# Two delta-net convolution tiles in place of two z tiles in a mixer's lead GEMM, with the delta net's gates woven beside the other convolutions

## The chip, the cores and the metric

The kernel runs on one core of a Trainium2 chip. A core has TensorE (PE; its weight loads are listed apart as PEld), VectorE (DVE), ScalarE (ACT), GpSimd (POOL) and SyncE (SP), which in this kernel issues transfers only. The metric is the device time of one execution in microseconds (us), as a median over runs. The compiler lays out each engine's instructions in one queue ahead of time, and an engine takes its queue in order.

## The reference, cut to what matters

The network takes 512 tokens of width 1024 and has four layers: two of a first kind, each a mixer and a feed-forward part, and two of a second kind, which the change doesn't touch. A mixer is, cut:

```python
h = rmsnorm(x, norm_mix_g[l])
proj = h @ w_in[l]
(qa, ka, va, qd, kd, vd, beta_logit, decay_logit, z, gate_logit) = jnp.split(proj, offsets, axis=-1)
...
y_attn = grid_attention(qa, ka, va) @ w_o_attn[l]
qkv = jax.nn.silu(centred_depthwise_conv(jnp.concatenate([qd, kd, vd], axis=-1), dn_conv_w[l])).astype(f32)
...
beta = jax.nn.sigmoid(beta_logit.astype(f32)).reshape(b, s, 2, DN_HEADS)
g = -jnp.exp(dn_a_log[l].astype(f32)) * jax.nn.softplus(
    decay_logit.astype(f32).reshape(b, s, 2, DN_HEADS) + dn_dt_bias[l].astype(f32))
o = bidir_gated_deltanet(qd, kd, vd, beta, g)
o = rmsnorm(o, dn_out_norm_g[l]) * jax.nn.silu(z.astype(f32).reshape(b, s, DN_HEADS, DN_DV))
y_dn = o.reshape(b, s, DN_V).astype(x.dtype) @ w_o_dn[l]
gates = jax.nn.sigmoid(gate_logit).reshape(b, s, N_BRANCH, D_MODEL)
mixed = gates[:, :, 0] * y_attn + gates[:, :, 1] * y_dn
```

So z (512 columns, four tiles of 128) and the 2048 gate columns (sixteen tiles) are needed only at the end of a mixer, while the convolution of qd, kd, vd (1536 columns, twelve tiles) and beta and g (32 columns) are what the delta net begins with.

## The kernel before, in words

**GEMMs.** Activations lie feature by token. Every GEMM splits its operands in a high and a low part and makes three products. `wload` (L390) brings a weight tile from HBM to `st`; ScalarE copies the high part `wh`; VectorE, or for a share given by `aid` GpSimd, subtracts to `wl`. `g_fm` (L414) makes one PSUM tile of 128 features by 512 tokens with 24 matmuls (8 steps along the width of 1024, three products each), after each step yields a cost of 0.64, and at the end calls an evacuation. Its PSUM tiles come from the pool `pg` with three banks, and with one bank during the scan (`share_banks`, L135, which also finishes a background tile that was begun).

**Lead and follow.** The rms norm is one row R over the tokens, and it multiplies a GEMM's result rather than its input. So the first GEMM of a stage runs before R is known: `lead` (L177) takes two generators for eight steps each; `follow` (L195) runs them to their end, which is their evacuation. In a mixer the two are z tiles (`begin_mixer`, L1319; from `load_x` for the first layer, from the end of the FFN for the second), evacuated by `g_tanh` (L1254): tha = 0.5 * pg * R on VectorE, a tanh to thz on ScalarE, for z (but not for the gate tiles) a second VectorE operation, and a store from SP's queue.

**Background.** Tiles that are needed late are pushed on a list: the two other z tiles, then eight tiles `ga` and eight `gd` (L1339). `pull` adds the cost of each foreground step, times a ratio, to a debt, and steps the list while the debt is positive (L149 to L207). `pe` (L240) keeps background matmuls a fixed number of foreground instructions behind. `weave` (L219) interleaves streams by cost over weight.

**The delta net** (`delta_net`, L1272) has three stages:
- `prepare` runs with ratio R1[4] = 0.059, woven with the attention's row inputs (`g_grid_inputs`, weight R1[6] = 0.491). Within it come first the gates (`g_dn_gates`, L864: one GEMM of 32 columns into a `pg` bank, transposed products into `pa`, a softplus in many small VectorE operations, sums by small matmuls, gc, eg and kds, and a round trip through memory to the factors `fac`), then the convolutions of head group 0 (`g_dn_inputs`, L947; q, k, v of two tiles each), then those of group 1 woven with the decay tiles (`g_dn_decay`, L991, which read `fac`).
- the solve of both groups (`g_dn_solve`, L1012) runs with ratio R1[1] = 0.633.
- the scan of both groups and the attention run with ratio R1[2] = 0.45 and one `pg` bank.

After that all remaining background is run, and the output GEMMs follow.

**A convolution tile's evacuation** (`evac`, L956): VectorE writes pad = pg * R into one of two pad buffers, which frees the bank; ScalarE starts the sum (cva, a scaled copy); VectorE adds the four other taps (cva from pad, cols, cva); ScalarE takes a tanh (cvt); VectorE joins them (cva from cvt, cva); TensorE transposes four times into `pt`; ScalarE copies to the q, k or v tile; for q and k ScalarE squares and VectorE reduces (dnms). When all six tiles of a group are done, dnv and a short chain of small operations give the l2 norm's factor, and tmk and tmq are scaled.

R1 (L1904) = [2.071, 0.633, 0.45, 3.49, 0.059, 9.505, 0.491, 4.55, 0.469, 0.387, 0.519, 0.788]; the last three are GpSimd's shares of `wl` (for foreground and background up to the solve, and for background in it). The change leaves R1 as it is.

Of the kernel before, what the change touches and what calls it, by code (L numbers as in the profile page):

```python
# [11 lines left out]
AF = mybir.ActivationFunctionType  # L12
ALU = mybir.AluOpType
AX = mybir.AxisListType
# [5 lines left out]
T = 512  # L20
D = 1024
NT = 4
# [84 lines left out]
class Net:  # L107
    def __init__(self, tc, I, consts, out):
        self.tc, self.nc, self.I, self.out = tc, tc.nc, I, out
        self.consts = consts  # L110
        nc = tc.nc
        self.V, self.G, self.S, self.PE = nc.vector, nc.gpsimd, nc.scalar, nc.tensor
        self.n = 0
# [830 lines left out]
        self.act(gt, p4, AF.Exp)  # L944
        return beta3, fac, kds3, eg3, gt

    def g_dn_inputs(self, l, pool, ip, g):  # L947

        w = self.I["w_in"][l]
        out = {}  # L950
        ms = self.t(self.sm, [128, 2, NT, 4], "dnms")
        for kind in range(3):
            dst = self.t(pool, [128, NT, 256], "tm" + "qkv"[kind], bufs=2)
            out["qkv"[kind]] = dst

            def evac(i, ps, kind=kind, dst=dst):  # L956
                ft = 4 * kind + 2 * g + i
                c = [self.cols[:, 64 + 60 * l + 12 * j + ft : 65 + 60 * l + 12 * j + ft] for j in range(5)]
                p = self.pad[self.npad % 2]
                self.npad += 1  # L960
                self.tt(p[:, 2 : T + 2], ps, self.R, ALU.mult)
                a = self.t(ip, [128, T], "cva")
                self.act(a, p[:, 2 : T + 2], AF.Copy, scale=c[2])
                for j in (0, 1, 3, 4):
                    self.stt(a, p[:, j : j + T], c[j], a, ALU.mult, ALU.add)
                th = self.t(ip, [128, T], "cvt")
                self.act(th, a, AF.Tanh, scale=0.5)
                self.stt(a, th, 1.0, a, ALU.add, ALU.mult)
                pt = self.t(self.pt, [128, T], "pt")
                for t in range(NT):  # L970
                    self.tr(pt[:, 128 * t : 128 * t + 128], a[:, 128 * t : 128 * t + 128])
                p3 = pt.rearrange("p (t n) -> p t n", t=NT)
                self.act(dst[:, :, 128 * i : 128 * i + 128], p3, AF.Copy, scale=0.5 if kind == 2 else 1.0)
                if kind < 2:
                    sq = self.t(ip, [128, T], "cvt")
                    self.act(sq, pt, AF.Square)
                    self.V.tensor_reduce(ms[:, kind, :, 2 * i : 2 * i + 2],
                                         sq.rearrange("p (t h d) -> p t h d", t=NT, h=2), AX.X, ALU.add)

            yield from self.g_fm(w, D, 768 + 512 * kind + 256 * g, 256, self.xh, self.xl, evac, 128)  # L980
        v = self.small(32, "dnv", 2)
        self.V.tensor_scalar(v, ms.rearrange("p a t h -> p (a t h)"), 4 * EPS, None, ALU.add)
        r = self.small(32, "dnr", 2)
        self.rsqrt(r, v)
        self.V.tensor_scalar(r[:, 0:16], r[:, 0:16], 0.125, None, ALU.mult)
        for kind in range(2):
            a = out["qkv"[kind]].rearrange("p t (h d) -> p (t h) d", d=64)
            self.tt(a, a, bc(r[:, 16 * kind : 16 * kind + 16], 64), ALU.mult)
        return out
# [282 lines left out]
    def delta_net(self, l, od, inputs, attention):  # L1272

        pool, cm = self.pool(f"dn{l}", bufs=2)
        ep, ecm = self.pool(f"dne{l}", bufs=4, side="right")
        ip, icm = self.pool(f"dni{l}", bufs=4)

        def prepare():  # L1280
            G = yield from self.g_dn_gates(l, pool, ep, ip)
            x0 = yield from self.g_dn_inputs(l, pool, ip, 0)
            x1, E0, E1 = yield from self.weave(
                (self.g_dn_inputs(l, pool, ip, 1), 1.0), (self.g_dn_decay(l, ep, 0, G), R1[0]),
                (self.g_dn_decay(l, ep, 1, G), R1[0]),
            )
            return G, (x0, x1), (E0, E1)

        self.aid = R1[9], R1[10]
        (G, x, E), _ = self.run(prepare(), R1[4], (inputs, R1[6]))  # L1290
        icm.__exit__(None, None, None)
        self.aid = 0.0, R1[11]
        tp, tcm = self.pool(f"dnt{l}", bufs=2)
        sp, scm = self.pool(f"dns{l}", bufs=2)
        sol = self.run(
            self.g_dn_solve(l, tp, ep, sp, 0, x[0], E[0]), R1[1],
            (self.g_dn_solve(l, tp, ep, sp, 1, x[1], E[1]), 1.0),
        )
        for c in (scm, ecm):
            c.__exit__(None, None, None)  # L1300
        cp, ccm = self.pool(f"dnc{l}", bufs=2)
        ap, acm = self.pool(f"ga{l}", bufs=2)
        hp, hcm = self.pool(f"gh{l}", bufs=2, side="right")
        self.aid = 0.0, 0.0
        self.share_banks(True)
        self.pull(R1[8])
        _, _, oa = self.run(
            self.g_dn_scan(l, cp, 0, x[0], G, *sol[0], od), R1[2],
            (self.g_dn_scan(l, cp, 1, x[1], G, *sol[1], od), 1.0), (attention(ap, hp), R1[3]),
        )  # L1310
        self.share_banks(False)
        for c in (acm, ccm, tcm, cm):
            c.__exit__(None, None, None)
        return oa, hcm
# [3 lines left out]

    def begin_mixer(self, l):  # L1319
        self.zd = self.t(self.dr, [128, 4, T], f"zd{l}")  # L1320
        z = self.tanh_tiles(self.I["w_in"][l], 2336, 4, lambda f: self.zd[:, f, :], True)
        self.push("z", *z[2:])
        return [(g, 8) for g in z[:2]]

    def mixer(self, l):
        self.last = deque(self.last, maxlen=LAG[0])
        I = self.I
        w = I["w_in"][l]
        thd = self.t(self.dr, [128, 16, T], f"thd{l}")
        zd = self.zd  # L1330
        ad = self.t(self.dr, [128, 4, T], f"ad{l}")
        qd = self.t(self.dr, [128, 4, 2, T], f"qd{l}")
        kd = self.t(self.dr, [128, 2, 2, T], f"kd{l}")
        vd = self.t(self.dr, [128, 2, NT, 2, 64], f"vd{l}")
        gp, gcm = self.pool(f"mix{l}", bufs=2)
        self.gp = gp
        od = [self.t(gp, [128, 2, T], f"o{g}", bufs=1) for g in range(2)]
        self.follow()
        self.push("ga", *self.tanh_tiles(w, 2848, 8, lambda f: thd[:, f, :]))  # L1339
        self.push("gd", *self.tanh_tiles(w, 2848 + 1024, 8, lambda f: thd[:, 8 + f, :]))  # L1340

        def gate(f, ps, dst):
            th = self.t(dp, [128, T], "th", bufs=4)
            self.nc.sync.dma_start(th, thd[:, f, :])
            self.stt(dst, th, 1.0, ps, ALU.add, ALU.mult)

        inputs = self.g_grid_inputs(l, qd, kd, vd)
        oa, hcm = self.delta_net(l, od, inputs, lambda pool, hp: self.g_grid_attention(l, pool, hp, qd, kd, vd, ad))
        for name in ("z", "ga", "gd"):
            self.need(name)  # L1350
        pool, cm = self.pool(f"mo{l}", bufs=2)
        mx = self.f32r_tiles(pool, NK, "m")
        dp, dcm = self.pool(f"md{l}", bufs=2)
        self.selp = self.t(dp, [128, 4, 128], "selp", F32R, bufs=1)
        self.V.tensor_copy(self.selp.rearrange("p a b -> p (a b)"), self.const(dp, "selp", 128, 512, "sq"))
        o = self.f32r_tiles(dp, 4, "o")
        u = [self.t(dp, [128, T], f"u{f}", bufs=1) for f in range(NK)]

        def evac_d(f, ps):
            a = self.t(dp, [128, T], "sq")  # L1360
            gate(8 + f, ps, a)
            self.tt(a, a, u[f], ALU.add)
            self.split(mx[0][f], mx[1][f], a)


        norm = self.g_dn_out(l, dp, zd, od, o)
        part = self.g_fm(I["w_o_attn"][l], 512, 0, D, *oa, lambda f, ps: gate(f, ps, u[f]), 128)
        for n in (4, 8, 4):
            for _ in range(n):
                next(part)  # L1370
            self.after = next(norm)
        self.run(norm)
        self.run(part)
        self.after = None
        self.gemm_fm(I["w_o_dn"][l], 512, 0, D, *o, evac_d)
        dcm.__exit__(None, None, None)
        hcm.__exit__(None, None, None)
        self.residual(pool, I["w_out"][l], D, *mx, 0.5, self.col(1, l), lambda: self.begin_ffn(l))
        for c in (cm, gcm):
            c.__exit__(None, None, None)  # L1380
# [523 lines left out]
R1 = [2.071, 0.633, 0.45, 3.49, 0.059, 9.505, 0.491, 4.55, 0.469, 0.387, 0.519, 0.788]  # L1904
# [54 lines left out]
```

## Time and profile before

| | |
|---|---|
| median of 3 runs | 3095.34 us (3093.31 to 3095.86) |
| the profiled execution | 3096.09 us, of which its span is 3094.3 |
| mean granted TensorE clock of the profiled execution | 0.988 |
| PE, DVE, ACT, POOL busy, share of the span | 97%, 72%, 49%, 13% |

The profile is one execution of its own, 0.75 us above the median. Its times are in us unless marked ns; durations of matmuls overlap, since they are pipelined. A name such as pad or cva is a tile of the program; "out<-in" says what an instruction writes and reads; L254, L257 and L260 are the helpers through which all VectorE and ScalarE operations pass, so the tile tells them apart and not the line. The granted clock is a share of full speed.

### The profile page before, as it was taken

What the parts mean: (1) busy time and instruction counts of PE and PEld (TensorE: products, weight loads), DVE (VectorE), ACT (ScalarE), POOL (GpSimd) and SP (SyncE); (2) the same over time, 40 slices, a digit from 0 to 9 for tenths busy, and PEclk for the clock granted to TensorE, in tenths of its full rate; (3) what the DMA queues carried; (4) which work ended last, traced back from release to release, by engine and by line L of the source; (5) the groups of instructions that cost most, each with busy time, mean ns of one, the idle gap of its engine ahead of it and who ended that gap; (6) DMA issues with size and microseconds to landing.
All of it is one profiled execution on the core that took longest, in us unless ns stands there. A gap on an engine that the chain in (4) does not pass through costs nothing. (4 is left out here: it accounts for less than half of the span.)

```text
span 3094.3 us, 54458 instructions
## 1 busy us (share of the span) xinstructions
PE 3011.5 (97%) x20148; PEld 2540.6 (82%) x20148; DVE 2221.3 (72%) x4974; ACT 1502.0 (49%) x3043; POOL 416.4 (13%) x550
## 2 busy tenths in 40 slices
PE   8989999999999899999999999999999999999999
PEld 6877778888888777788888898888888898878977
DVE  5988776777448887777774466778686666788684
ACT  3544744444324456544443344366464453476463
POOL 2433300000014343100000000200100010200200
PEclk9999999999999999999999999999999999999999
DMA  4435125333343342253333454522435545422525
GB/s 146 115 90 146 43 88 175 96 99 96 125 129 89 106 120 85 68 167 107 98 98 123 136 140 131 143 75 73 123 113 186 158 118 150 121 66 67 162 87 183
DMA packets 403116, 359.02 MB, mean 116 GB/s; under 512 B 32867, under 2 KB 350307, under 8 KB 402851
## 3 DMA queue, kind: packets, MB, share of 16 engines
q1 hardware_dynamic: 396707, 335.62, 37.6%
q0 software_dynamic: 6144, 19.93, 1.8%
q8 instruction: 159, 2.61, 0.4%
q14 instruction: 106, 0.87, 0.1%
HBM read 293.98 MB, written 61.47 MB: 115 GB/s over the span
## 5 line engine op out<-in xcount | busy, mean ns | idle before, releaser
L260 ACT ACTIVATE wh<-st 128x512 fp32r<-128x512 f32 x844 | 528.2, 629 | 788.5 <-PE pg L238 633.4
L254 DVE TENSOR_TENSOR wl<-st,wh 128x512 fp32r<-128x512 f32 x766 | 539.0, 705 | 402.0 <-ACT wh L260 397.2
L238 PE MATMUL pg<-xh,wh 128*128 128x512 f32 (+1 forms) x1824 | 733.0, 402 | 3.6 <-ACT wh L260 2.2
L238 PE MATMUL pg<-xh,wl 128*128 128x512 f32 (+1 forms) x1824 | 719.9, 395 | 5.3 <-POOL wl L254 5.3
L238 PE MATMUL pg<-xl,wh 128*128 128x512 f32 (+1 forms) x1824 | 712.2, 395 | 0.0
L238 PEld LDWEIGHTS pg<-xl,wh 128*128 128x128 f32 (+1 forms) x1824 | 343.4, 188 | 73.8 <-issue 0.4
L238 PEld LDWEIGHTS pg<-xh,wl 128*128 128x128 f32 (+1 forms) x1824 | 344.2, 189 | 72.0 <-POOL wl L254 7.0
L238 PEld LDWEIGHTS pg<-xh,wh 128*128 128x128 f32 (+1 forms) x1824 | 344.2, 189 | 70.7 <-ACT wh L260 2.6
L238 PE MATMUL pg<-wl,xh 128*128 128x256 f32 x928 | 265.1, 287 | 0.4 <-DVE wl L254 0.4
L238 PE MATMUL pg<-wh,xh 128*128 128x256 f32 x928 | 262.6, 287 | 1.1 <-DVE oz L257 0.8
L238 PE MATMUL pg<-wh,xl 128*128 128x256 f32 x928 | 263.0, 285 | 0.0
L238 PEld LDWEIGHTS pg<-wh,xh 128*128 128x128 f32 x928 | 176.3, 192 | 6.2 <-DVE oz L257 1.0
L238 PEld LDWEIGHTS pg<-wl,xh 128*128 128x128 f32 x928 | 177.9, 192 | 3.9 <-DVE wl L254 0.8
L238 PEld LDWEIGHTS pg<-wh,xl 128*128 128x128 f32 x928 | 177.7, 192 | 1.2
L485 POOL DMA_DIRECT2D xd<-xn x40 | 21.8, 544 | 1049.5 <-DVE xn L257 927.5
L254 POOL TENSOR_TENSOR wl<-st,wh 128x512 fp32r<-128x512 f32 x78 | 123.1, 1584 | 267.5 <-ACT wh L260 234.4
L238 PE MATMUL pg<-hh,wl 128*128 128x512 f32 x352 | 137.0, 389 | 0.0
L238 PE MATMUL pg<-hh,wh 128*128 128x512 f32 x352 | 136.7, 389 | 0.0
L238 PE MATMUL pg<-hl,wh 128*128 128x512 f32 x352 | 135.7, 389 | 0.0
L260 ACT ACTIVATE p<-pa,anb 128x128 f32<-128x128 f32 (+1 forms) x224 | 115.6, 517 | 36.9 <-DVE anb L725 34.0
L257 DVE SCALAR_TENSOR_TENSOR u<-pad,cols,u 128x512 f32<-128x512 f32 x176 | 127.3, 746 | 0.7
L260 ACT ACTIVATE ph<-pt 128x128 fp32r<-128x128 f32 (+1 forms) x224 | 94.9, 426 | 65.9 <-PE pt L251 64.5
(509 smaller groups left out, 6276.2 us busy)
## 6 DMA issues: line engine op xcount, KB each, us to landing
st<-in_w_in_dram SPq DMA_DIRECT2D x400, 256.0 KB
st<-in_w_up_dram SPq DMA_DIRECT2D x176, 256.0 KB
st<-in_w_down_dram SPq DMA_DIRECT2D x88, 256.0 KB
st<-in_w_out_dram SPq DMA_DIRECT2D x64, 256.0 KB
xo<-xd SPq DMA_DIRECT2D x48, 256.0 KB
th<-thz SPq DMA_DIRECT2D x48, 256.0 KB
xd<-xn POOLq DMA_DIRECT2D x40, 256.0 KB, 4.0
thd<-thz SPq DMA_DIRECT2D x32, 256.0 KB
```

The source lines that it names most:

```text
L238: return self.pe(self.PE.matmul(out, lhsT, rhs, start=start, stop=stop, **kw))
L254: return (eng or self.V).tensor_tensor(out, a, b, op)
L257: return self.V.scalar_tensor_tensor(out, a, s, b, op0, op1)
L260: return self.S.activation(out, in_, f, **kw)
L485: self.nc.gpsimd.dma_start(self.xd[:, k, :], x)
```

## The change

- The lead GEMM of a mixer is two convolution tiles (q, tiles 0 and 1, which are head group 0's), not two z tiles. All four z tiles go to the background list, ahead of the gate tiles.
- The evacuation of a convolution tile and its GEMM become a function of their own, `g_conv`; `dn_tiles` makes a group's tiles. `g_dn_inputs` leaves out the first `led` tiles.
- `follow()` moves from `mixer` into `delta_net`, behind the opening of its pools, and so behind the pushing of the gate tiles.
- The gates are no longer run ahead of group 0's convolutions, but woven beside the four that are left, with weight 0.8 against 1.0.

```diff
-    def g_dn_inputs(self, l, pool, ip, g):
+    def g_conv(self, l, kind, f, dst, ms):
+        def evac(_, ps):
+            ft = 4 * kind + f
...
+            p = self.pad[self.npad % 2]
+            self.npad += 1
+            self.tt(p[:, 2 : T + 2], ps, self.R, ALU.mult)
+            a = self.t(self.conv_pool, [128, T], "cva")
...
         w = self.I["w_in"][l]
-        out = {}
-        ms = self.t(self.sm, [128, 2, NT, 4], "dnms")
+        return self.g_fm(w, D, 768 + 512 * kind + 128 * f, 128, self.xh, self.xl, evac, 128)
+
+    def dn_tiles(self, pool, g):
+
+        x = {k: self.t(pool, [128, NT, 256], "tm" + k, bufs=2) for k in "qkv"}
+        return x, self.t(self.sm, [128, 2, NT, 4], "dnms")
+
+    def g_dn_inputs(self, l, g, tiles, led=0):
+
+
+        out, ms = tiles
         for kind in range(3):
...
-            yield from self.g_fm(w, D, 768 + 512 * kind + 256 * g, 256, self.xh, self.xl, evac, 128)
+            for i in range(2):
+                if 2 * kind + i >= led:
+                    yield from self.g_conv(l, kind, 2 * g + i, lambda kind=kind: out["qkv"[kind]], lambda: ms)
...
         ip, icm = self.pool(f"dni{l}", bufs=4)
+        self.conv_pool = ip
+        self.conv_tiles = self.dn_tiles(pool, 0)
+        self.follow()
 
         def prepare():
-            G = yield from self.g_dn_gates(l, pool, ep, ip)
-            x0 = yield from self.g_dn_inputs(l, pool, ip, 0)
+            x0, G = yield from self.weave(
+                (self.g_dn_inputs(l, 0, self.conv_tiles, 2), 1.0), (self.g_dn_gates(l, pool, ep, ip), 0.8)
+            )
             x1, E0, E1 = yield from self.weave(
-                (self.g_dn_inputs(l, pool, ip, 1), 1.0), (self.g_dn_decay(l, ep, 0, G), R1[0]),
+                (self.g_dn_inputs(l, 1, self.dn_tiles(pool, 1)), 1.0), (self.g_dn_decay(l, ep, 0, G), R1[0]),
                 (self.g_dn_decay(l, ep, 1, G), R1[0]),
             )
...
         self.zd = self.t(self.dr, [128, 4, T], f"zd{l}")
-        z = self.tanh_tiles(self.I["w_in"][l], 2336, 4, lambda f: self.zd[:, f, :], True)
-        self.push("z", *z[2:])
-        return [(g, 8) for g in z[:2]]
+        self.push("z", *self.tanh_tiles(self.I["w_in"][l], 2336, 4, lambda f: self.zd[:, f, :], True))
+        lead = lambda i: self.g_conv(l, 0, i, lambda: self.conv_tiles[0]["q"], lambda: self.conv_tiles[1])
+        return [(lead(i), 8) for i in range(2)]
...
         od = [self.t(gp, [128, 2, T], f"o{g}", bufs=1) for g in range(2)]
-        self.follow()
         self.push("ga", *self.tanh_tiles(w, 2848, 8, lambda f: thd[:, f, :]))
```

## Rows read from the trace of the kernel before

**Rows 1.** The page: busy time, share and instructions of each engine.

```profile
PE 3011.5 (97%) x20148; PEld 2540.6 (82%) x20148; DVE 2221.3 (72%) x4974; ACT 1502.0 (49%) x3043; POOL 416.4 (13%) x550
```

**Rows 2.** Stages: us, busy PE, PEld, DVE, ACT, POOL, clock, DMA share, GB/s.

```profile
45.50:201.00 155.50, 146.19 (x848) 122.12 (x849) 136.14 (x266) 71.09 (x128) 62.58 (x53) 0.95 0.35 100
201.00:303.00 102.00, 96.92 (x1126) 78.53 (x1125) 84.17 (x181) 49.07 (x78) 36.42 (x28) 0.97 0.45 121
303.00:430.00 127.00, 124.06 (x1817) 99.29 (x1815) 95.03 (x255) 82.83 (x198) 33.57 (x64) 1.00 0.15 48
...
906.90:1066.00 159.10, 149.09 (x877) 124.26 (x876) 133.49 (x268) 72.90 (x130) 59.04 (x54) 0.96 0.36 101
1066.00:1168.00 102.00, 98.89 (x1153) 80.23 (x1151) 85.75 (x184) 49.05 (x79) 38.92 (x28) 0.98 0.45 127
1168.00:1293.00 125.00, 122.30 (x1794) 98.23 (x1795) 93.43 (x249) 81.82 (x196) 33.56 (x64) 1.00 0.15 45
```

**Rows 3.** Windows: opening and rest of both preparations.

```profile
45.50:75.00 29.50, 28.74 (x200) 24.83 (x201) 18.84 (x39) 8.96 (x17) 4.30 (x3) 0.88 0.27 75
75.00:201.00 126.00, 117.45 (x655) 97.29 (x653) 117.29 (x228) 62.13 (x111) 58.27 (x50) 0.96 0.37 106
906.90:945.00 38.10, 38.10 (x284) 32.86 (x283) 22.10 (x45) 13.96 (x28) 4.27 (x4) 0.96 0.30 84
945.00:1066.00 121.00, 111.00 (x594) 91.40 (x594) 111.39 (x224) 58.94 (x103) 54.77 (x50) 0.96 0.38 107
```

**Rows 4.** Timeline of DVE from 45.5 us: start, duration, instruction [idle before <-releaser].

```profile
45.52 0.69 DVE L257 SCALAR_TENSOR_TENSOR tha<-pg,R 128x512 f32<-128x512 f32 x1 [1.74 <-ACT R L260]
...
57.67 0.69 DVE L254 TENSOR_TENSOR pad<-pg,R 128x512 f32<-128x512 f32 x1
...
67.01 0.23 DVE L896 COPY gc<-pa 128x64 f32<-128x64 f32 x1 [2.31 <-PE pa L238]
...
70.07 0.75 DVE L257 SCALAR_TENSOR_TENSOR cva<-pad,cols,cva 128x512 f32<-128x512 f32 x1
```

**Rows 5.** Timeline of ACT in the same stretch.

```profile
67.27 0.26 ACT L260 ACTIVATE eg<-gc 128x64 f32<-128x64 f32 x1 [3.30 <-DVE gc L896]
...
69.23 0.71 ACT L260 ACTIVATE cva<-pad,cols 128x512 f32<-128x512 f32 x1
```

**Rows 6.** Windows of 5 us at the end of the first preparation.

```profile
185.00:190.00 5.00, 0.82 (x4) 0.71 (x4) 4.47 (x7) 2.45 (x5) 0.00 (x0) 0.65 0.41 115
190.00:195.00 5.00, 2.41 (x9) 1.80 (x8) 4.63 (x14) 2.71 (x5) 0.00 (x0) 0.50 0.49 199
```

**Rows 7.** Waits of PE, 0 to 480 us: who for whom, total, times, longest.

```profile
PE pt L251 <- DVE hl L254: 4.9, 1, 4.9
...
PE pt L251 <- DVE dnv L982: 2.6, 1, 2.6
```

**Rows 8.** Windows: a stretch of plain GEMMs in a later layer.

```profile
700.00:750.00 50.00, 50.00 (x222) 41.45 (x221) 38.11 (x59) 23.52 (x38) 0.00 (x0) 1.00 0.35 96
```

**Rows 9.** Groups of DVE, 45.5 to 201 us: busy, mean ns, idle before.

```profile
L257 DVE SCALAR_TENSOR_TENSOR cva<-pad,cols,cva 128x512 f32<-128x512 f32 x48 | 39.8, 832 | 2.2 <-ACT cva L260 1.6
L254 DVE TENSOR_TENSOR wl<-st,wh 128x512 fp32r<-128x512 f32 x22 | 17.1, 782 | 3.8 <-ACT wh L260 3.7
L257 DVE SCALAR_TENSOR_TENSOR cva<-cvt,cva 128x512 f32<-128x512 f32 x12 | 9.4, 781 | 0.3 <-ACT cvt L260 0.2
L254 DVE TENSOR_TENSOR pad<-pg,R 128x512 f32<-128x512 f32 x12 | 8.2, 687 | 3.2 <-PE pg L238 2.9
L977 DVE TENSOR_REDUCE dnms<-cvt 128x8 f32<-128x512 f32 x8 | 5.5, 682 | 0.8 <-ACT cvt L260 0.7
...
L257 DVE SCALAR_TENSOR_TENSOR thz<-thz,tha 128x512 f32<-128x512 f32 x4 | 3.8, 958 | 0.8 <-ACT thz L260 0.7
...
L257 DVE SCALAR_TENSOR_TENSOR tha<-pg,R 128x512 f32<-128x512 f32 x4 | 2.8, 688 | 2.0 <-ACT R L260 1.7 <-PE pg L238 0.2
```

**Rows 10.** Waits of DVE, 906.9 to 1066 us.

```profile
DVE pad L254 <- PE pg L238: 5.2, 2, 4.9
```

More of the change, by code (lines that the diff above doesn't have):

```diff
@@ L945, in g_dn_gates @@
         return beta3, fac, kds3, eg3, gt
-    def g_dn_inputs(self, l, pool, ip, g):
-        w = self.I["w_in"][l]
-        out = {}
-        ms = self.t(self.sm, [128, 2, NT, 4], "dnms")
-        for kind in range(3):
[L953 to L978, printed above, removed]
-            yield from self.g_fm(w, D, 768 + 512 * kind + 256 * g, 256, self.xh, self.xl, evac, 128)
@@ new lines, in g_conv @@
+    def g_conv(self, l, kind, f, dst, ms):
+        def evac(_, ps):
+            ft = 4 * kind + f
+            c = [self.cols[:, 64 + 60 * l + 12 * j + ft : 65 + 60 * l + 12 * j + ft] for j in range(5)]
+            p = self.pad[self.npad % 2]
+            self.npad += 1
+            self.tt(p[:, 2 : T + 2], ps, self.R, ALU.mult)
+            a = self.t(self.conv_pool, [128, T], "cva")
+            self.act(a, p[:, 2 : T + 2], AF.Copy, scale=c[2])
+            for j in (0, 1, 3, 4):
+                self.stt(a, p[:, j : j + T], c[j], a, ALU.mult, ALU.add)
+            th = self.t(self.conv_pool, [128, T], "cvt")
+            self.act(th, a, AF.Tanh, scale=0.5)
+            self.stt(a, th, 1.0, a, ALU.add, ALU.mult)
+            pt = self.t(self.pt, [128, T], "pt")
+            for t in range(NT):
+                self.tr(pt[:, 128 * t : 128 * t + 128], a[:, 128 * t : 128 * t + 128])
+            p3 = pt.rearrange("p (t n) -> p t n", t=NT)
+            i = f % 2
+            self.act(dst()[:, :, 128 * i : 128 * i + 128], p3, AF.Copy, scale=0.5 if kind == 2 else 1.0)
+            if kind < 2:
+                sq = self.t(self.conv_pool, [128, T], "cvt")
+                self.act(sq, pt, AF.Square)
+                self.V.tensor_reduce(ms()[:, kind, :, 2 * i : 2 * i + 2],
+                                     sq.rearrange("p (t h d) -> p t h d", t=NT, h=2), AX.X, ALU.add)
+        w = self.I["w_in"][l]
+        return self.g_fm(w, D, 768 + 512 * kind + 128 * f, 128, self.xh, self.xl, evac, 128)
```

## The prediction, made before the changed kernel was run

> **What bounds the kernel now.** I read the page's totals first: TensorE holds 3011.5 of the 3094.3 us span [rows 1], so nothing gains much unless TensorE's holes are closed, and work that it merely does at another time costs the same there. Next the busy time by stage of each mixer [rows 2]. A mixer has three: the preparation of the delta net (45.5 to 201 us in the first layer, 906.9 to 1066 in the second), the solve (102 us each), and the scan with the attention (127 and 125 us). TensorE stands idle for 155.50 - 146.19 = 9.3 and 159.10 - 149.09 = 10.0 us in the preparations, 5.1 and 3.1 in the solves, 2.9 and 2.7 in the scans. VectorE is loaded the other way: 136.14 of 155.50 us and 133.49 of 159.10 in the preparations, 84 to 86 of 102 in the solves, 95 of 127 in the scans. So the preparation is the one stage with two near bounds, and the rest is TensorE's.
>
> Then the preparation in two parts [rows 3]. In its opening VectorE is busy for 18.84 of 29.50 us and 22.10 of 38.10: idle 10.7 and 16.0. In what follows it is busy for 117.29 of 126.00 and 111.39 of 121.00: idle 8.7 and 9.6 only. Its timeline says why [rows 4]: the norm row is there at 45.5 us, the two lead tiles z are evacuated, then come the gates' small operations, and the first long conv operation starts at 70.07, though the conv tile's first step (pad) was done at 57.67. ScalarE's timeline shows what lay between: the copy that opens the conv (cva) ran at 69.23, behind the gates' exponential eg, for which ScalarE had idled 3.30 us waiting on VectorE's gc [rows 5]. TensorE pays at the far end: at 185 to 195 us it is busy for 0.82 and 2.41 of 5 us at a granted clock of 0.65 and 0.50 [rows 6], and its two long waits there are for VectorE (hl 4.9 us, dnv 2.6 us) [rows 7]. VectorE idles early and is late at the end.
>
> **The change, part by part.** *TensorE's work* stays the same in sum. A tile of 24 matmuls costs 24 x 50.00 / 222 = 5.4 us in an undisturbed GEMM stretch [rows 8]; I take 5.5. Lead for lead is nothing. Before, two conv tiles lay in the preparation that now lie in the lead: -11.0 us of TensorE there in each layer.
>
> *Where the z tiles go.* Background steps are paid by foreground cost times a ratio. From the code: preparation 106.88 x 0.059 = 6.31, solve 120.42 x 0.633 = 76.23, sum 82.53, in tiles of 8 x 0.64 = 5.12: sixteen and a begun seventeenth, which the change of banks finishes. After, the preparation counts two conv tiles less, 96.64 x 0.059 = 5.70, sum 81.93, which is just over 81.92: again seventeen. Of 18 pushed tiles 1 was left for the scan; of 20 now, 3 are. Two tiles more in the scan, +11.0 us, since TensorE idles only 2.9 and 2.7 us there: the work has no hole to hide in. There the tiles share one bank instead of three, so each waits for its evacuation: bounded by nothing (other matmuls stand in between) and by one evacuation (688 ns) and a wait for it per tile; I take the far end, 1.0 us a layer. The scan's debt allows the three tiles early (208 x 0.45 = 94 of cost against 15), so nothing is left over when it ends. The last gate tile's store leaves some 12 us later than before, early in a stage of over 120 us after which its reader comes: nothing.
>
> *Solve.* Two of its seventeen tiles are now z tiles, each with the longer second operation (958 ns, which a tile of the gates ga and gd doesn't have) [rows 9], and their two stores go through SP's queue. 2 x 0.69 = 1.4 us of VectorE undisturbed, 1.9 at the mean; VectorE idles 17.8 us there, and TensorE sets the end. I take nothing, and 1.9 if that cover fails.
>
> *Preparation, by VectorE.* It loses two z evacuations: 2 x (688 + 958) ns = 3.3 us at the means [rows 9], 2.8 at the 0.69 that such an operation takes undisturbed [rows 4]; I take 2.8. The weight splits of two conv tiles move ahead of it, two of 128x512 to a tile; VectorE has 0.61 of them (the code gives POOL 0.387), at 782 ns [rows 9]: 4 x 0.61 x 0.78 = 1.9. Together -4.7. The conv evacuations all stay (one is 687 + 4 x 832 + 781 + 682 ns = 5.5 us [rows 9]), but three of them can start when the norm row lands, since three banks hold two led tiles and the next. That is 16 us of work for an opening hole of 10.7 and 16.0. If the hole fills and the later idle (8.7, 9.6) stays, the preparation ends 4.7 + 10.7 = 15.4 us earlier in the first layer and 20.7 in the second. *By TensorE:* 146.19 - 11.0 - 1 (the few matmuls at the half rate, 1.2 instead of 2.4 GHz [rows 6]) plus 5 us that stay idle in the tail, where the chain of the last normalisation runs without it: 139 us, against 140.1 by VectorE; second layer 149.09 - 12 + 5 = 142.1, against 138.4. The later one counts: -15.4 and -17.0.
>
> *The gates beside the convolutions.* The gates' GEMM yields 5.12 of cost at weight 0.8, so the chain is issued after some 6.4 of the 20.48 that the four other tiles of the first group cost, 14 before the decays that read its factors. Their round trip through memory stays covered. If it isn't, the decays are late by what is lacking; bounded by the 12 us that the chain took to gc before (55 to 67 us), I take nothing. The row stages of the attention, woven at 0.491, end at 62.6 of 76.2 units before and of 65.9 after: more crowded at the end, less tail. Nothing, with the tail's 5 us as its measure.
>
> **The sum.** -15.4 - 17.0 + 2 x (11.0 + 1.0) = -8.4. The profiled execution took 3096.09 us (span 3094.3), 0.75 over the median of 3095.34; 3096.09 - 8.4 = 3087.7, so **3088 us**, 7.3 below the median. Two runs of this kernel can be told apart from about 0.2%, 6.2 us: the forecast is just outside. Its own range is 3079 to 3089: the low end where the preparations gain 15.4 and 20.7, nothing is waited for on the one bank, and 2 of TensorE's 5 us of tail go too in the first layer (-17.4 - 20.7 + 22.0 = -16.1 and 3080, rounded down), the high end where the solve's cover fails in one layer (1.9).
>
> **The rivals.** *The hole only moves (same).* VectorE is in order; the gates' chain of some twenty short dependent operations now falls between convolutions, and a conv's own chain waits for ScalarE twice (cva, cvt). If 7.3 us of the hole are filled in each layer, the 4.7 + 7.3 = 12.0 pay the scan's 12.0 and no more: 3096. Between 5 and 10 us filled lies 3091 to 3101. For it: the second layer's pad waits of 5.2 us for TensorE [rows 10] show that the hole is partly a lack of finished GEMMs, and they do not come sooner for being woven.
>
> *The scan pays, the preparation doesn't (slower).* If the gates keep their place ahead on ScalarE's queue, as in [rows 5], the conv copies stand behind eg as now and the third pad waits for one of two pad buffers. Its place is between 46 and 70 us; it decides below 7.3 us filled. With 4 filled: +3.3 x 2, 3102.7; with none: +14.6, 3110.7. Against it: the led tiles' convolutions are issued ahead of the gates, by follow(), so at least their ten long operations have nothing but R to wait for.
>
> *The scan takes the two tiles for less (faster still).* By the trace the scan's TensorE is busy for 124.06 of 127.00 us, but its weight loads only for 99.29, 78%, where a plain GEMM stretch has 41.45 of 50.00, 83% [rows 2, 8]. Were the scan to run as densely as that stretch, it would do its present work in 99.29 / 0.829 = 119.8 us, 7.2 less, and 6.5 less in the second layer: 3088 - 13.7 = 3074. Against it: small foreground matmuls wait for each other there, and their ends, not a lack of issue, fill the time.
> The Trainium skill (Perfetto Trace Analysis, Identifying the Most-Contended Engine) says that matmul busy time misjudges how much room TensorE has, since pipelined matmuls look otherwise in the trace, and that the busy share of weight loads tells it better. By that rule the scan has the room of this rival, and by the busy time it has 3; no row of before decides it.
>
> **The chances.** Forecast 0.42, the denser scan 0.05, the hole that moves 0.32, the slower case 0.21. Faster by over 0.2% (below 3089.1) 0.47, within 0.2% 0.32, slower (above 3101.5) 0.21. Range: 3074 takes in the denser scan; at the top I go to 3106, which holds the moved hole and the slower case down to 2.3 us filled, and leaves out the rest of it.
>
> **What to look for afterwards.** The first long conv operation on VectorE at about 47 us instead of 70; VectorE's opening 29.5 us busy for over 24; the end of the preparation (the last tmq) near 185 and 1049; TensorE's waits for hl and dnv shrunk; three background tiles after the scan begins, and a scan of about 139 us. A scan still near 127 speaks for the denser scan; a preparation shorter by under 12 us for one of the two other rivals. The forecast is wrong if the z tiles land elsewhere than in the scan, or if VectorE's hole moves into the middle of the preparation instead of closing.

## The result, and the profile after

The changed kernel takes 3128.78 us (median of 4 runs, 3118.04 to 3133.60) against 3095.60 before: ratio 1.0104, interval 1.0075 to 1.0133. It is slower, by 33 us, outside the forecast's range and beyond every rival that it named. The profiled execution took 3132.47 us, 3.7 over its median; its page, beside [rows 1]:

```profile
span 3130.7 us, 54486 instructions
...
PE 3032.3 (97%) x20148; PEld 2550.3 (81%) x20148; DVE 2216.8 (71%) x4977; ACT 1505.8 (48%) x3043; POOL 404.0 (13%) x547
```

TensorE has the same 20148 matmuls as before. Of the 36.4 us that the span grew, 20.8 are busy time (3011.5 to 3032.3) and 15.6 idle (82.8 to 98.4).

To compare stages, marks are needed that mean the same work in both kernels. I take: the norm row R; the last l2 scaling (tmq), where the preparation ends; the first and the last matmul that multiplies by the scan's state (qf,S); and the R of the feed-forward part (FFN). Where the second stretch is split, the first matmul into as, the attention's scores, marks the end of the solve and the beginning of the scan. The windows between these marks, of both mixers, first of the kernel before (columns as in [rows 2]):

```profile
44.89:200.64 155.75, 145.83 (x847) 121.83 (x848) 136.14 (x266) 71.69 (x129) 62.22 (x53) 0.95 0.35 99
200.64:329.96 129.32, 124.21 (x1466) 99.48 (x1464) 100.64 (x220) 67.64 (x122) 42.11 (x38) 0.97 0.41 114
329.96:427.79 97.83, 95.70 (x1460) 77.53 (x1463) 76.80 (x211) 63.59 (x152) 28.24 (x55) 1.00 0.12 36
427.79:544.42 116.63, 112.73 (x522) 93.24 (x519) 77.25 (x148) 44.66 (x74) 4.92 (x9) 0.96 0.55 168
906.30:1066.83 160.53, 150.53 (x883) 125.44 (x882) 134.32 (x268) 73.50 (x131) 60.47 (x54) 0.96 0.36 101
1066.83:1193.52 126.69, 123.55 (x1467) 99.22 (x1465) 100.49 (x220) 67.25 (x122) 43.41 (x38) 0.99 0.41 117
1193.52:1292.03 98.51, 95.84 (x1461) 77.64 (x1464) 76.98 (x211) 63.62 (x152) 28.25 (x55) 1.00 0.12 35
1292.03:1408.28 116.25, 112.46 (x522) 93.02 (x519) 77.24 (x148) 44.66 (x74) 4.92 (x9) 0.96 0.55 169
```

and of the changed kernel:

```profile
44.01:185.93 141.92, 129.96 (x786) 106.84 (x785) 124.47 (x257) 65.29 (x117) 49.74 (x46) 0.97 0.33 93
185.93:339.98 154.05, 145.72 (x1551) 114.50 (x1551) 113.25 (x238) 76.28 (x138) 48.91 (x44) 0.97 0.39 112
339.98:440.34 100.36, 96.62 (x1455) 76.92 (x1456) 73.03 (x201) 62.97 (x150) 26.66 (x53) 1.00 0.12 36
440.34:559.51 119.17, 115.03 (x515) 95.43 (x512) 77.41 (x149) 43.75 (x72) 4.92 (x9) 0.93 0.53 164
920.43:1062.20 141.77, 132.68 (x816) 109.68 (x814) 126.02 (x258) 66.26 (x119) 51.45 (x47) 0.99 0.35 97
1062.20:1216.72 154.52, 146.58 (x1551) 116.21 (x1551) 111.17 (x238) 76.52 (x138) 49.01 (x44) 0.96 0.38 112
1216.72:1320.38 103.66, 99.53 (x1453) 79.54 (x1455) 73.28 (x201) 63.10 (x150) 26.63 (x53) 0.97 0.12 35
1320.38:1439.79 119.41, 115.34 (x515) 95.63 (x512) 77.53 (x149) 43.57 (x72) 4.92 (x9) 0.93 0.53 163
```

The preparation is shorter by 13.8 and 18.8 us, near the 15.4 and 17.0 of the forecast. All of it and more comes back between its end and the first scan step: +24.7 and +27.8. The scan's steps add 2.5 and 5.2, what follows 2.5 and 3.2. The sums, 16.0 and 17.4 a mixer, make 33.4 of the 36.4; 4.8 more lie behind the second mixer's FFN norm row, in work that the change doesn't touch, and are not explained (elsewhere 1.8 was won).

The forecast's sign of the first step was seen. VectorE's timeline of the changed kernel, where [rows 4] had the first long conv operation at 70.07:

```profile
44.64 1.29 DVE L254 TENSOR_TENSOR pad<-pg,R 128x512 f32<-128x512 f32 x2 [0.17 <-ACT R L260]
46.12 5.76 DVE L257 SCALAR_TENSOR_TENSOR cva<-pad,cols,cva 128x512 f32<-128x512 f32 x7 [0.19 <-ACT cva L260]
...
85.48 0.23 DVE L896 COPY gc<-pa 128x64 f32<-128x64 f32 x1 [2.02 <-PE pa L238]
```

It now starts at 46.12, and gc, the end of the gates' chain, has gone from 67.01 to 85.48. The windows of the changed kernel's preparation, beside [rows 3, 6]:

```profile
45.50:75.00 29.50, 27.68 (x162) 21.48 (x162) 25.16 (x52) 12.76 (x25) 5.54 (x4) 1.00 0.27 72
75.00:100.00 25.00, 23.31 (x190) 20.09 (x189) 17.84 (x47) 8.60 (x18) 9.26 (x12) 0.93 0.29 75
...
170.00:186.00 16.00, 7.82 (x36) 5.70 (x34) 14.68 (x35) 5.22 (x10) 5.56 (x6) 0.86 0.26 66
```

VectorE's opening hole is mostly filled (busy for 25.16 of 29.50 us, 18.84 before), a new one of 7.2 us stands at 75 to 100, where the gates' chain now is, and TensorE's hole at the end is still there: 8.2 us idle of the last 16, where it was 6.8 of 16 before (185 to 201 us).

Where the z tiles went: the evacuations of background tiles in the changed kernel's scan (VectorE's timeline, cut to the tile tha), and the scan's first step (TensorE's):

```profile
306.39 0.69 DVE L257 SCALAR_TENSOR_TENSOR tha<-pg,R 128x512 f32<-128x512 f32 x1 [1.86 <-PE pg L238]
...
319.16 0.69 DVE L257 SCALAR_TENSOR_TENSOR tha<-pg,R 128x512 f32<-128x512 f32 x1 [3.00 <-PE pg L238]
...
334.12 0.69 DVE L257 SCALAR_TENSOR_TENSOR tha<-pg,R 128x512 f32<-128x512 f32 x1 [0.72 <-PE pg L238]
```

```profile
339.98 0.50 PE L238 MATMUL pt<-qf,S 64*64 64x64 f32 x5
```

The kernel before had one there. That tile and its first step:

```profile
311.42 0.69 DVE L257 SCALAR_TENSOR_TENSOR tha<-pg,R 128x512 f32<-128x512 f32 x1 [0.79 <-PE pg L238]
```

```profile
329.96 0.50 PE L238 MATMUL pt<-qf,S 64*64 64x64 f32 x5
```

Three tiles, as the debt arithmetic said, but 12.8 and 15.0 us apart, where a plain GEMM stretch makes one in 5.4. They are the last of the list, gate tiles: all z tiles go ahead of them. The attention's first matmul of the scan stands at 302.18 us after and 307.88 before; from there to the first step it is 37.8 us against 22.1.

### The profile page after: what moved, and what is told of

It is laid out like the page before. It is cut to its first block, busy times and chain, and to the rows that moved or that the text cites. A ratio compares the mean times of both kernels' runs of the same rounds, so it can differ in the third digit from the quotient of the medians.

```text
span 3130.7 us, 54486 instructions
## 1 busy us (share of the span) xinstructions
PE 3032.3 (97%) x20148; PEld 2550.3 (81%) x20148; DVE 2216.8 (71%) x4977; ACT 1505.8 (48%) x3043; POOL 404.0 (13%) x547
## 5 line engine op out<-in xcount | busy, mean ns | idle before, releaser
L254 POOL TENSOR_TENSOR wl<-st,wh 128x512 fp32r<-128x512 f32 (+1 forms) x75 | 121.3, 1625 | 234.5 <-ACT wh L260 224.2
```

The source lines that it names most:

```text
L254: return (eng or self.V).tensor_tensor(out, a, b, op)
```

## The experiments

Two theories at first: A, the tiles in the scan are dear; B, the woven gates are at fault. A third, C, came from what the first of them showed. Each run is beside the kernel before on the same chip (3095.5 to 3095.8 us there). All need the same work; "left" is the number of background tiles left for the scan, by the code; in every trace as many evacuations (tha) lie between the first attention matmul and the last scan step of each mixer.

| run | lead | gates | left | us | ratio (interval) |
|---|---|---|---|---|---|
| before | z | first | 1 | 3095.6 | |
| changed | conv | woven | 3 | 3128.8 | 1.0104 (1.0075 to 1.0133) |
| e1 | conv | first | 3 | 3116.0 | 1.0071 (1.0049 to 1.0092) |
| e2 | z | woven | 1 | 3103.4 | 1.0025 (1.0016 to 1.0035) |
| e3, solve 0.72 | conv | woven | 1 | 3106.5 | 1.0034 (1.0022 to 1.0046) |
| e4, solve 0.547 | z | first | 3 | 3111.0 | 1.0053 (1.0036 to 1.0070) |
| e5, preparation 0.167 | conv | woven | 1 | 3101.5 | 1.0022 (1.0012 to 1.0031) |
| e6, scan 0.08 | conv | woven | 3 | 3123.4 | 1.0093 (1.0078 to 1.0108) |
| e7, preparation 0.167 | conv | first | 1 | 3102.9 | 1.0023 (1.0013 to 1.0032) |
| e8, solve 0.68 | z | first | 0 | 3107.3 | 1.0041 (1.0030 to 1.0053) |
| e9, two pulled behind | conv | first | 1 | 3093.4 | 0.9989 (0.9979 to 0.9998) |
| e10, two pulled behind | conv | woven | 1 | 3091.1 | 0.9989 (0.9980 to 0.9999) |
| e11, two pulled behind | z | first | 1 | 3098.5 | 1.0013 (1.0003 to 1.0022) |
| e12, two pulled ahead | conv | first | 1 | 3085.9 | 0.9972 (0.9960 to 0.9983) |
| e13, two pulled ahead | conv | woven | 1 | 3091.1 | 0.9988 (0.9979 to 0.9998) |
| e14, one pulled ahead | conv | first | 2 | 3103.6 | 1.0025 (1.0014 to 1.0035) |
| e15, three pulled ahead | conv | first | 0 | 3095.0 | 0.9992 (0.9978 to 1.0006) |

**e1: gates first.** On the changed kernel:

```diff
-            x0, G = yield from self.weave(
-                (self.g_dn_inputs(l, 0, self.conv_tiles, 2), 1.0), (self.g_dn_gates(l, pool, ep, ip), 0.8)
-            )
+            G = yield from self.g_dn_gates(l, pool, ep, ip)
+            x0 = yield from self.g_dn_inputs(l, 0, self.conv_tiles, 2)
```

> The changed kernel with its conv lead kept, but the gates run ahead of group 0's convolutions again, not woven. Theory A (the loss is the two background tiles that now run in the scan on one bank, some 9 to 10 us each instead of 5.5, and a preparation and solve that give back 4 to 6 us instead of the 11 that left them): the scan stays at 127 to 131 us, the time within 8 us of the changed kernel, 3120 to 3135. Theory B (the weave is at fault: the gates' chain ends late and the decays and the solve with it): most of the loss goes, at or under 3108, and the solve is back at 105 to 107 us from the last tmq to the first as.

Between the two: by the medians 13 us of the 33 go and 20 stay. The 13 rest on four runs each, whose ranges overlap (3110.3 to 3127.1 here, 3118.0 to 3133.6 for the changed kernel); the 20 are clear. The stretch from the last tmq to the first scan step stays long.

```profile
43.82:180.81 136.99, 127.23 (x774) 107.11 (x774) 123.11 (x257) 65.16 (x118) 52.24 (x46) 0.97 0.34 96
180.81:334.11 153.30, 145.55 (x1550) 114.52 (x1550) 113.34 (x238) 76.19 (x138) 49.10 (x44) 0.97 0.39 113
...
914.09:1055.09 141.00, 132.37 (x812) 110.80 (x810) 123.07 (x258) 66.46 (x120) 56.82 (x47) 0.98 0.35 98
1055.09:1207.59 152.50, 144.72 (x1550) 114.60 (x1550) 111.19 (x238) 76.43 (x138) 48.90 (x44) 0.97 0.39 113
```

153.30 and 152.50 against 129.32 and 126.69 before: not the weave's doing.

**e3 and e4: two tiles out of the scan, and two into it.** e3 is the changed kernel, e4 the kernel before:

```diff
-R1 = [2.071, 0.633, 0.45, 3.49, 0.059, 9.505, 0.491, 4.55, 0.469, 0.387, 0.519, 0.788]
+R1 = [2.071, 0.72, 0.45, 3.49, 0.059, 9.505, 0.491, 4.55, 0.469, 0.387, 0.519, 0.788]
...
+R1 = [2.071, 0.547, 0.45, 3.49, 0.059, 9.505, 0.491, 4.55, 0.469, 0.387, 0.519, 0.788]
```

> The changed kernel with the solve's background ratio 0.72 in place of 0.633, so that by its code 19 of the 20 background tiles are done before the scan and 1 is left in it, as before the change. Theory A: the scans fall back by 18 to 21 us each to 108 to 110, the solves grow by 11 to 12, and the time falls to 3108 to 3118. Theory B, or that a tile costs the same in either place: 3124 to 3135.

> The kernel before with the solve's ratio 0.547 in place of 0.633: by its code 15 of 18 tiles are done before the scan and 3 are left in it, as in the changed kernel; nothing else differs from before. Theory A: the scans grow by 18 to 21 us each and the solves shrink by 11: slower by 14 to 20, 3110 to 3116. If a tile in the scan costs what it costs elsewhere: 3093 to 3100, and the loss of the changed kernel lies in the preparation and solve.

e3 wins 22 us back, a little more than A said. e4 loses 15 with nothing changed but the place of two tiles: the total that A named, though not stage by stage. Its first two stages in each mixer:

```profile
44.45:196.17 151.72, 140.72 (x824) 117.15 (x825) 133.71 (x264) 69.42 (x126) 58.45 (x49) 0.96 0.35 99
196.17:335.25 139.08, 130.61 (x1501) 103.92 (x1500) 107.76 (x231) 72.92 (x131) 42.56 (x39) 0.98 0.39 109
...
908.41:1066.62 158.21, 147.17 (x863) 122.14 (x862) 131.90 (x266) 71.50 (x128) 57.11 (x50) 0.96 0.36 101
1066.62:1205.99 139.37, 130.79 (x1501) 104.02 (x1499) 107.82 (x231) 72.81 (x131) 42.49 (x39) 0.98 0.38 109
```

The preparation gives back 4.0 and 2.3 us, TensorE's idle time in the second stretch grows from 5.1 and 3.1 to 8.5 and 8.6. The narrower stretch from the last tmq to the scan's first attention matmul, the solve, took 102.8 and 103.1 us against 107.2 and 104.6 before. So two tiles taken out ahead of the scan save 8.5 and 3.9 us there and not 11: TensorE idles instead. From that matmul to the scan's last step it took 138.8 and 140.4 us against 119.9 and 120.6, that is 18.9 and 19.8 for the two tiles, of which 7.9 and 5.9 come back behind the last step (108.8 and 110.3 us to the FFN's R, 116.6 and 116.3 before).

**e5 and e7: the two tiles into the preparation,** spread over it, e5 on the changed kernel and e7 on e1 (0.059 becomes 0.167 in R1).

> The changed kernel with the preparation's background ratio 0.167 in place of 0.059: 19 of 20 tiles done before the scan, and the two extra ones in the preparation, where the two conv tiles were: TensorE's work by stage is then as before the change, and only the lead, the order and the weave differ. Theory A: scan back at 108 to 110 us, and the preparation 0 to 6 us shorter than before since VectorE's opening hole is filled: 3085 to 3105. Theory B: the late decays stay, solve over 112 us, 3108 to 3120.

> Conv lead, gates ahead of the other convolutions as before, and the preparation's ratio 0.167, so that one tile is left for the scan. Theory A and the weave's price add up: 3101.5 less some 6 to 13, so 3088 to 3096, at or under the kernel before. If the weave's price was only paid through the scan's crowding: 3098 to 3104.

Both recover most of the loss (3101.5, 3102.9); the scans are back (from the first to the last step 97.8 to 98.4 us in all four), but neither beats the kernel before, although TensorE's work by stage is nearly as in it and part of VectorE's opening hole is filled. e7 fell on the second line of its expectation.

**e2: the weave alone,** on the kernel before, with the same edit as e1 the other way round.

> The kernel before, with its z lead, and only the gates woven (weight 0.8) beside group 0's six convolutions instead of ahead of them. If the weave costs by itself what it seemed to cost beside the conv lead (3128.8 against 3116.0 without it, 13 us): 3102 to 3110, with gc some 40 us after R instead of 20. If it only costs where the led convolutions fill VectorE first: 3093 to 3099. That the second theory is wholly right, and the weave gains here: below 3090.

3103.4, at the low end of the first line: the weave costs 7.9 us by itself. gc came 36.7 and 41.9 us after R (22.1 and 20.4 before), the preparations took 158.6 and 165.0 us.

**e6: the three tiles spread over the scan** (0.45 becomes 0.08 in R1, on the changed kernel).

> The changed kernel with the scan's background ratio 0.08 in place of 0.45: its three tiles are spread over the whole scan instead of coming in its first sixth. If the price of a tile in the scan comes from its crowding the start on one bank: 3108 to 3120, scans 115 to 120 us. If it is TensorE's own time in the scan: 3122 or more. Third possibility, a bank held long by a slow tile delays the scan's own use of it: over 3135.

3123.4, as the second line says: crowding of the scan's start is not the price, or at most some 5 us of it, which the spread of the changed kernel's runs doesn't tell from nothing.

**e8: no tile left for the scan,** on the kernel before (0.633 becomes 0.68).

> The kernel before with the solve's ratio 0.68 in place of 0.633: all 18 background tiles are done before the scan, none is left in it. If each tile in the scan costs 3.8 us more than elsewhere (two tiles were 7.6 a mixer): 3086 to 3090, faster. If the first tile fits into the scan's start for nothing: 3094 to 3106, since the solve grows by 5.5 a mixer.

3107.3, 12 us slower: the first tile does fit into the scan for nothing (121.4 and 120.1 us without it from the first attention matmul to the last step, 119.9 and 120.6 with it), and taking it out hurts by more than I had allowed. That made theory C: a background tile is a filler. What counts is where TensorE would stand idle for a chain, and a tile taken from there or put elsewhere costs.

**e9 to e12: two tiles pulled in one piece at the end of the preparation,** where most of the 8 to 13 us lie that TensorE idles in the preparation of every kernel so far. e9 (on e1), e10 (on the changed kernel) and e11 (on the kernel before, with 0.548 for the solve) pull behind group 1's last convolution, e12 (on e1) ahead of it. e12's edit, and e9's (e10 has the same, e11 the like in the kernel before):

```diff
                 if 2 * kind + i >= led:
+                    if not led and kind == 2 and i == 1:
+                        self.pull(10.3)
                     yield from self.g_conv(l, kind, 2 * g + i, lambda kind=kind: out["qkv"[kind]], lambda: ms)
...
                     yield from self.g_conv(l, kind, 2 * g + i, lambda kind=kind: out["qkv"[kind]], lambda: ms)
+        if not led:
+            self.pull(10.3)
```

> Conv lead, gates ahead, ratios of the changed kernel, and 10.3 of background cost (two tiles) pulled in one piece behind the last convolution of group 1: 19 of 20 tiles before the scan, the two extra ones aimed at the hole of some 10 us that TensorE keeps at the end of the preparation. Theory C (the loss is that too little background is issued where the dependent chains leave TensorE idle, and that the hole at the preparation's end is such a place): the preparation grows by less than 6 us over that without the pull (137 and 141), the scans are back at 98, the time falls to 3075 to 3092, below the kernel before. If the hole at the end is VectorE's (it is busy for 9 of 10 us there), the tiles' own splits and evacuations prolong it: 3096 to 3106, as with the two tiles spread over the preparation.

> The same pull in the changed kernel, gates woven. Theory C: 3082 to 3100, some 7 to 13 us above the kernel with the gates ahead. If the hole at the end is VectorE's: 3100 to 3112.

> The kernel before with the same pull and the solve's ratio 0.548, so that as many tiles are done before the scan as in it and two move from the solve into the end of the preparation. If that hole takes tiles for nothing and the solve gives back what they cost there: 3075 to 3090. Since the solve gave back only 4 us of 11 for two tiles taken out of it: 3090 to 3100.

> Conv lead, gates ahead, the pull ahead of the last convolution of group 1 and not behind it. If the place of the two tiles decides (they now run before TensorE's last convolution and delay it, and the hole behind stays): 3098 to 3108. If it doesn't: the same as with the pull behind, within 4 us.

e10 takes 38 us off the changed kernel with one call. e9 is just above C's line, e11 as its second line says. e12 fits neither line: ahead of the last convolution is better by 7.5 us, and it beats both kernels. The kernel before was not run with the pull at that place, so how much of the 9.7 us by which e12 beats it belongs to the convolution lead is open. Its windows, to be read against e1's, from which it differs by that call alone:

```profile
44.28:178.58 134.30, 132.92 (x801) 112.76 (x802) 121.05 (x254) 63.96 (x116) 51.55 (x46) 0.97 0.35 100
178.58:323.45 144.87, 135.72 (x1511) 108.97 (x1510) 111.54 (x232) 75.08 (x135) 50.25 (x45) 0.95 0.40 117
...
899.16:1036.34 137.18, 136.03 (x839) 115.03 (x838) 120.62 (x255) 65.59 (x118) 57.28 (x47) 1.00 0.36 102
1036.34:1182.96 146.62, 134.92 (x1512) 108.74 (x1510) 111.59 (x233) 75.42 (x135) 49.60 (x45) 0.97 0.40 116
```

The preparation has 27 matmuls more than e1's in each mixer and is shorter by 2.7 and 3.8 us: its idle time on TensorE went from 9.8 and 8.6 to 1.4 and 1.2. The next stretch is shorter by 8.4 and 5.9, though part of the hole comes back in it: TensorE idles there for 9.2 and 11.7 us, 7.8 and 7.8 in e1.

**e13, e14, e15: the weave once more, and one or three tiles pulled,** at e12's place (e13 on the changed kernel; e14 and e15 are e12 with 5.2 and 15.4).

> The changed kernel, gates woven, with the pull of two tiles ahead of the last convolution. If the weave has a price of its own: 3092 to 3100, 6 to 13 us above the same with the gates ahead (3085.9). If its price was only paid where TensorE ran out of tiles: 3083 to 3089.

> Conv lead, gates ahead, one tile (5.2 of cost) pulled ahead of the last convolution: 18 of 20 before the scan, 2 left in it. If each tile moved out of the scan into the preparation's end is worth the same: halfway between 3116.0 and 3085.9, 3098 to 3104. If the second tile in the scan is nearly free: 3085 to 3092.

> The same with three tiles (15.4 of cost): all 20 before the scan, none in it. If a tile there is worth 15 us as from 0 to 2: 3070 to 3078. If the scan's first tile fills a hole of the scan's own, as emptying it did in the kernel before (11 us lost): 3090 to 3100.

e13 falls between its two lines: against e12 the weave costs 5.1 us here, short of the 6 to 13 named. e14 and e15 came out as the first and the second of their lines. By the number left for the scan the time goes 3116.0 (3), 3103.6 (2), 3085.9 (1), 3095.0 (0): some 12 and 18 us for each tile taken out of the scan into the preparation's end, and 9 lost with the last, as 12 in e8. The first mixer's scan, from its first attention matmul to its last step, with no tile (e8) and with two (e14), to be read beside 119.91 us with one (before) and 138.16 with three (changed kernel), both shown below:

```profile
313.79:435.14 121.35, 114.47 (x1756) 91.93 (x1755) 89.75 (x245) 81.12 (x192) 33.32 (x64) 0.97 0.11 34
```

```profile
301.40:429.23 127.83, 122.50 (x1788) 97.00 (x1788) 92.74 (x247) 84.86 (x197) 33.98 (x64) 1.00 0.13 40
```

In this stretch the first tile costs nothing, the second 7.9 us and the third 10.3. The steps of e15's scan show what is lost without the first:

```profile
331.55:431.58 100.03, 93.89 (x1461) 75.67 (x1462) 76.71 (x210) 65.75 (x153) 26.37 (x52) 1.00 0.12 36
...
1191.01:1295.35 104.34, 97.79 (x1460) 78.61 (x1462) 76.83 (x210) 65.79 (x153) 26.36 (x52) 0.95 0.11 34
```

As many matmuls as in the scan before, but 6.1 and 6.5 us idle and not 2.1 and 2.7. Not all of e15's loss against e12 is this: in its profiled execution one stretch ran at a low granted clock (last section).

## Why the prediction was wrong

**What bounds the kernel.** It read VectorE's opening hole as the cause of TensorE's hole at the end. The opening hole of the first mixer shrank from 10.7 us to 4.3 in the changed kernel, 5.6 in e1 and 7.2 in e7, and TensorE's idle time in the two preparations stayed: 9.9 and 10.0 before; 12.0 and 9.1 after; 9.8 and 8.6 in e1; 11.9 and 11.2 in e7. The hole at the end is the last convolutions' chain with no matmuls issued beside it: e12 closed it with background tiles.

**The preparation.** -15.4 and -17.0 forecast, -13.8 and -18.8 measured: the size was near, the working was not, and that is luck in part. TensorE's busy time there fell by 15.9 and 17.9 us, with the matmuls that left; its idle time changed by +2.0 and -0.9, where the prediction had it about halved. In the first mixer VectorE's idle time fell by 2.2 us (19.6 to 17.4) and not 10.7; its busy time fell by 11.7 and not 4.7, in part since work of the row inputs slid behind the last tmq. In VectorE's groups of the first preparation, of before and after:

```profile
L254 DVE TENSOR_TENSOR hl<-pt,hl 64x512 fp32r<-64x512 f32 x8 | 5.4, 687 | 0.2
```

```profile
L254 DVE TENSOR_TENSOR hl<-pt,hl 64x512 fp32r<-64x512 f32 x5 | 3.4, 687 | 0.2
```

TensorE lost 61 and 67 matmuls there, not the 48 of two tiles. Those 13 and 19 had still to be done.

**The failed step: "Two tiles more in the scan, +11.0 us", with 1.0 for the shared bank, and "I take nothing" for the solve.** Together that is 12.0 a mixer. From the preparation's end to the first scan step alone, +24.7 and +27.8 were measured. The solve, and the scan from its first attention matmul to its last step, in the first mixer of before and of after:

```profile
200.64:307.88 107.24, 102.16 (x1162) 82.61 (x1161) 86.14 (x186) 50.76 (x81) 36.78 (x28) 0.97 0.47 130
307.88:427.79 119.91, 117.76 (x1764) 94.40 (x1765) 91.30 (x244) 80.48 (x194) 33.57 (x64) 1.00 0.12 36
```

```profile
185.93:302.18 116.25, 107.95 (x1183) 87.04 (x1183) 91.27 (x190) 52.93 (x85) 41.93 (x32) 0.96 0.45 127
302.18:440.34 138.16, 134.40 (x1823) 104.39 (x1823) 95.01 (x249) 86.31 (x202) 33.64 (x64) 1.00 0.14 44
```

The solve grew by 9.0 us (12.1 in the second mixer) where nothing was taken, and the scan by 18.3 (20.9) where 12.0 was (the prediction's scan of 139 us is counted from an earlier mark, with 127 before). Up to the first step 85 and 84 matmuls more ran (48 of the two tiles, 13 and 19 deferred ones, the rest from ahead of R or from later), 19 us at the plain 0.225 us each [rows 8]. TensorE's idle time grew by 3.2 and 4.8 us, and its busy time by 21.5 and 23.0 for those 19 us of work; in the second mixer the granted clock of the stretch also fell, from 0.99 to 0.96. The error of method: tiles were priced by their matmuls at a plain stretch's rate in the place where they land, and a shortening was credited in full where they leave. e4 shows that even without the change two tiles cost 15 us for their place alone.

**What was not in the sum.** What follows the scan, +2.5 and +3.2, and the scan's own steps, +2.5 and +5.2 (these lie within the 18.3 and 20.9). In the second mixer the steps ran at a granted clock of 0.97 and not 1.00. Behind the scan the granted clock is 0.93 against 0.96. Two windows of the changed kernel just behind its last scan step, and the second such window of before:

```profile
440.00:450.00 10.00, 5.86 (x41) 4.41 (x40) 6.28 (x16) 3.44 (x7) 0.53 (x1) 0.72 0.44 136
450.00:460.00 10.00, 10.00 (x41) 9.23 (x41) 4.13 (x18) 2.02 (x4) 0.00 (x0) 0.50 0.64 206
```

```profile
437.80:447.80 10.00, 10.00 (x51) 8.70 (x51) 4.96 (x20) 3.10 (x5) 0.00 (x0) 0.77 0.74 238
```

41 matmuls at 1.2 GHz in the time of 51. Why the lower level lasts longer here is open; e1, e12 and e15 have 0.96 in both mixers.

**The gates.** "I take nothing": e2 and e13 give 7.9 and 5.1 us for the weave, 2.6 to 4.0 a mixer, within the bound of 12. Beside three tiles in the scan the medians differ by 13, over runs that overlap; with two tiles spread over the preparation (e5, e7) or pulled behind the last convolution (e9, e10) no price can be told. Why it varies is open.

**The rivals.** None of them reached 3128.8; the slowest was 3110.7. The slower one was not what happened: its place was between 46 and 70 us, with the gates ahead on ScalarE's queue, and the conv ran at 46.12. "The hole only moves" was partly true (75 to 100 us), but gave a time of no change. The denser scan is refuted: from its first attention matmul to its last step the scan took 138.16 us and not 119.91, with weight loads for 104.39 us of it, 76%, against 94.40, 79%; in the stretch before the first step they took 114.50 of 154.05 us, 74%, against 99.48 of 129.32, 77%. The Trainium skill (Perfetto Trace Analysis, Identifying the Most-Contended Engine) names the busy share of weight loads as one of two measures of TensorE's room. By it there was room that two more tiles did not get: it didn't tell here how long the dependent chains would be held up. e8 and e15 show that one tile fits, and e14 that the second doesn't.

The top of the prediction's own range adds up to 3089.6 and not 3089; nothing rests on it.

## What to carry to other kernels

Background work that is paid by foreground cost moves when the foreground shrinks: count what each stage will hold after the edit, and move the ratios with it. Price a filler by the idle time it covers where it leaves and by the chain it delays where it lands, not by its own length. When an engine idles at the end of a stage, look first whether anything was issued there for it to do: here one call that issues two tiles at that point was worth 30 us (e1 to e12), some 13 of them for moving the tiles from the scan into the preparation at all (e1 to e7) and 17 for the place (e7 to e12). The reordering that was meant to close the hole did not close it.

## What was not expected of the hardware

The changed kernel's executions spread over 15.6 us (3118.04 to 3133.60), those of the kernel before over 2.8 in the same comparison and over 5.2 to 10.3 in the longer series beside the experiments (15 to 27 runs), with as many matmuls and weight loads. The mean granted clock of the changed kernel's four runs was 0.985, 0.988, 0.985 and 0.984, and the run with 0.988 is the shortest. e15's ten runs go from 3085.99 us at 0.989 to 3105.78 at 0.982. In its profiled execution the stretch from the first attention matmul to the first scan step, the same work in both mixers, stood so:

```profile
301.61:331.55 29.94, 27.61 (x295) 21.49 (x295) 13.87 (x37) 16.54 (x41) 6.80 (x13) 0.66 0.12 40
1171.23:1191.01 19.78, 18.90 (x298) 14.78 (x294) 13.56 (x36) 15.11 (x40) 6.84 (x13) 1.00 0.14 46
```

At a granted clock of 0.66 it took 10.2 us more than at 1.00. What set the clock there is open, and that the clock makes the spread of the other kernels was not tried.
